# Attention by blocks of 128 queries instead of units of 64, beside the projections on one core

## The chip, the cores and the metric

The kernel runs on one core of one Trainium2 chip. The metric is the device time of one execution in microseconds; the median of 3 runs before is 797.51 us (797.22 to 797.78). Engines are called as the profile calls them: PE multiplies matrices, DVE, ACT and POOL work on tiles, SP issues most of the DMAs.

## The reference, cut to what matters

One layer of a trunk: attention with a sliding window of 128 keys over 512 positions, 32 query heads of 64 in 4 groups that share keys and values, then a gated output product, then a second gated product with an embedding. All in float32.

```python
def swa_mixer(h, w_in, w_out, sinks, rel_bias):
    q, k, v, gate = jnp.split(h @ w_in, [...], axis=-1)
    ...                                   # 4 blocks of 128 queries, each sees 256 keys
    scores = einsum(q, kb) * HEAD_DIM ** -0.5 + bias
    scores = where(mask, scores, min)     # a query sees itself and the 127 keys before it
    m = maximum(scores.max(-1), sink)
    e = exp(scores - m)
    probs = e / (e.sum(-1) + exp(sink - m))
    out = einsum(probs, vb)
    return (out * silu(gate)) @ w_out

def reference(x, p, ...):
    x = x + swa_mixer(rmsnorm(x, norm_g), ...)
    emb = p @ ple_proj
    x = x + emb * sigmoid(rmsnorm(x, ple_norm) @ ple_gate)
    return rmsnorm(x, final_g)
```

## The kernel before, in words

Each float32 operand of a large product is split in a high and a low part (a cast on ACT, a subtraction on DVE), and each product is three matmuls of 128x128 weights with 512 columns (`mm3`, lines 126 to 128). The work has four stages: a first pass over the input that makes keys, values and the first two query projections (to 71 us), then 30 projections with attention beside them (to about 455 us), then the output product, then the second gated product.

A projection is 16 steps of three matmuls (`projections`, a generator: `next(proj)` issues one step). A tile of split weights serves 8 steps. `Weights.get` asks for the split two tiles ahead; `W.todo` holds the splits that were asked for and not issued yet (`_make`: the cast at line 109, the subtraction at line 110). There are three buffers of each. When a projection ends, its result has to leave its bank: three chores go to the list `chores`, for a query projection a scaling on DVE (L312), two casts on ACT (L321) and two subtractions on DVE (L319), for a gate a product on DVE (L600), a tanh on ACT (L601) and a product on DVE (L594). `idle` holds work without haste.

The list `kinds` sets the order of the 14 query and 16 gate projections; `q_at` gives the places of the query projections. Two of them make the queries `Q[d]` of four heads, and there are 8 such `d`.

Attention goes by units of 64 queries and four heads, 64 units in all. A unit passes three generators:

- `scores`: two score products on PE into a bank each (L462), the sink into the tile `t` on POOL (L474); then the bias added, both parts summed, the folded keys merged and the maximum taken on DVE (L487 to L491); then two exponentials on ACT (L495); then the reciprocal of the sums on DVE (L497); then two scalings on ACT that write the tile `pr` (L506).
- `turn`: two transposes of `pr` on PE (L515), a cast on ACT (L520) and a subtraction on DVE (L521) that split the result into `r`; then, but for the first units of a `d`, a masked copy `own` on POOL (L531) and a copy between its halves on ACT (L541).
- `weigh`: two or three value products on PE (L557, L559); after each second unit, two copies on ACT (L568) and two additions on DVE (L570) empty the bank `o` into `U`.

In this stage every engine's order is the order of the program text (`manual_schedule` for PE, SP, DVE, ACT and POOL), so each engine takes its instructions as the loop issues them. In iteration `i` of the loop (from L828) stand, in this order: transposes of unit i-2, value products of unit i-3, score products of unit i, the reciprocal and scalings of unit i-1, the sums of unit i. Then come about 7 projection steps, between which chores, exponentials and copies are issued. `sum_weights` issues the DMAs that add weight tiles for later stages, on SP and POOL.

The tiles `r`, `own` have two buffers, `t` and `pr` three. Of the eight banks, two each belong to projections (tag p), transposes (t), outputs (o) and scores.

Of the kernel before, what the change touches and what calls it, by code (L numbers as in the profile page):

```python
# [11 lines left out]
F32 = mybir.dt.float32  # L12
F32R = mybir.dt.float32r
AF = mybir.ActivationFunctionType
ALU = mybir.AluOpType
# [15 lines left out]
UNITS = S // HB  # L31
# [9 lines left out]
WARM = 24  # L41
XW = S + 1 + 768
# [13 lines left out]
def trunk_kernel(ctx: ExitStack, tc: tile.TileContext, a: dict):  # L56
# [11 lines left out]
    others = {"s": banks_s.enter_context(tc.tile_pool(name="psum_s", bufs=2, space=PSUM))}  # L68
# [112 lines left out]
    q_at = {int(0.5 + 3.516 * (c // 2)) - 3 + c % 2: c for c in range(2, PAIRS)}  # L181
# [214 lines left out]
    spsum = mid.enter_context(tc.tile_pool(name="psum_w", bufs=1, space=PSUM))  # L396
# [7 lines left out]
    U, T, PT, O, gates, biases = {}, {}, {}, {}, {}, {}  # L404
# [41 lines left out]
    def scores(i):  # L446

        d, g = divmod(i, UNITS)
        if g == 4 and d + 1 < TWOS:
            load_bias(d + 1)
        key = K[d // 2]

        s_ps = spsum.tile([P, 2, S], F32, tag="w", name=f"s{i}")
        number = [min(2 * g + u + 1, 5) * QB for u in range(2)]
        for u in range(2):
            first, n = max(2 * g + u - 4, 0) * QB, number[u]  # L460
            st = Q[d][:, 2 * g + u].rearrange("p h q -> p (h q)")
            nc.tensor.matmul(s_ps[:, u, : 2 * n], st, key[:, :, first : first + n], start=True, stop=True)  # L462
        W = KEYS + 2
        t = apool.tile([P, 2, W], F32, tag="t", name=f"t{i}", bufs=3)
        at = t[:, 0, 0:1]

        def two(of, stride, n):
            return bass.AP(tensor=at.tensor, offset=at.offset + of, ap=[at.ap[0], [stride, 2], [1, n]])

        late = QB if g >= 2 else 0  # L470
        seen = [t[:, 0, 0 : P + 1], t[:, 1, 1 + late : P + 2 + late] if late else t[:, 1, 0 : P + 1]]
        both = two(0, W + 1 + late if late else W, P + 1)
        pr = [t[:, u, 1 + late * u : 1 + late * u + P] for u in range(2)]
        nc.gpsimd.tensor_copy(two(0, W + W - 1 if late else W, 1), sinkb[:, d : d + 1].unsqueeze(1).to_broadcast([P, 2, 1]))  # L474
        for u, n in enumerate(number):
            if n < P:
                nc.gpsimd.memset(t[:, u, 1 + n : 1 + P], MASKED)
        yield
        bias = biases[d][:, ::-1]
        if g < 2:  # L480
            for u, n in enumerate(number):
                nc.vector.tensor_add(t[:, u, 1 : 1 + n], s_ps[:, u, :n], bias[:, KEYS - n :])
            for u, n in enumerate(number):
                nc.vector.tensor_add(t[:, u, 1 : 1 + n], s_ps[:, u, n : 2 * n], t[:, u, 1 : 1 + n])
        else:
            x = t[:, :, 1 : 1 + KEYS]
            nc.vector.tensor_add(x, s_ps[:, :, :KEYS], bias.unsqueeze(1).to_broadcast([P, 2, KEYS]))  # L487
            nc.vector.tensor_add(x, s_ps[:, :, KEYS : 2 * KEYS], x)
            nc.vector.tensor_max(two(1, W + P, QB), t[:, :, 1 : 1 + QB], t[:, :, 1 + P : 1 + KEYS])
        sm = apool.tile([P, 24], F32, tag="sm", name=f"sm{i}", bufs=4)  # L490
        nc.vector.tensor_reduce(sm[:, 0:2], both, axis=AX.X, op=ALU.max, negate=True)  # L491
        yield
        for u in range(2):
            su = seen[u]
            nc.scalar.activation(su, su, AF.Exp, bias=sm[:, u : u + 1], accum_out=sm[:, 2 + u : 3 + u])  # L495
        yield
        nc.vector.reciprocal(sm[:, 4:6], sm[:, 2:4])  # L497
        yield

        T[i] = apool.tile([P, 2, P], F32, tag="pr", name=f"pr{i}", bufs=3)  # L500
        for u in range(2):
            out, src = T[i][:, u], pr[u]
            if late and (g + u) % 2:
                out = out.rearrange("p (h k) -> p h k", h=2)[:, ::-1]
                src = src.rearrange("p (h k) -> p h k", h=2)
            nc.scalar.mul(out, src, sm[:, 4 + u : 5 + u])  # L506

    def turn(i):


        d, g = divmod(i, UNITS)
        pr = T.pop(i)
        pt = bank(f"pt{i}", "t")[:, :256]
        for u in range(2):
            nc.tensor.transpose(pt[:, u * P : (u + 1) * P], pr[:, u, :], ident)  # L515

        r = apool.tile([P, 2, 256], F32R, tag="r", name=f"r{i}", bufs=2)
        rh, rl = (r[:, l].rearrange("p (h u q) -> p u h q", h=4, u=2) for l in range(2))
        src = pt.rearrange("p (u h q) -> p u h q", u=2, h=4)
        nc.scalar.copy(rh, src)  # L520
        nc.vector.tensor_sub(rl, src, rh.bitcast(F32))  # L521
        yield
        own = None
        if g >= 2:
            own = apool.tile([P, 2, 256], F32R, tag="own", name=f"own{i}", bufs=2)
            rows = slice(0, P) if g % 2 else slice(0, HB)
            flat = lambda v: v[rows].rearrange("p l (u q) -> p (l u) q", q=HB)


            sign = -1 if g % 2 else 1  # L530
            nc.gpsimd.affine_select(  # L531
                out=flat(own), in_=flat(r).bitcast(F32), pattern=[[0, 8], [sign, HB]], compare_op=ALU.is_ge, fill=0.0,
                base=-HB - 1 if g % 2 else 0, channel_multiplier=-sign,
            )
        PT[i] = (r, own)
        yield
        if own is not None:
            here, there = slice(HB, P), slice(0, HB)
            if g % 2 == 0:
                here, there = there, here  # L540
            nc.scalar.copy(own[there, 0], own[here, 1].bitcast(F32))  # L541

    def weigh(i):

        d, g = divmod(i, UNITS)
        n, b = divmod(g, 2)
        kv = d // 2
        r, own = PT.pop(i)
        if g == 0:
# [3 lines left out]
        ops = O[d]  # L553
        out = ops[:, b].rearrange("p u e q -> p (u e q)")
        first = V[0 if n == 0 else n - 1 + b][:, kv]
        for low in range(2):
            nc.tensor.matmul(out, first, r[:, low], start=low == 0, stop=own is None and low == 1)  # L557
        if own is not None:
            nc.tensor.matmul(  # L559
                out, DV[:, n - 1, b, kv * 2 * HD : (kv + 1) * 2 * HD], own[:, 0], start=False, stop=True  # L560
            )
        yield
        if b:
            dst = U[d][:, :, n * P : (n + 1) * P].rearrange("p u (b q) -> p b u q", b=2)
            lower, upper = slice(0, 64), slice(64, 128)
            tmp = [apool.tile([P, 2, 2, HB], F32, tag=f"tmp{e}", name=f"tmp{e}_{i}", bufs=1) for e in range(2)]
            for e, (o, x) in enumerate(((lower, upper), (upper, lower))):
                nc.scalar.copy(tmp[e][o], ops[x, :, :, e, :])  # L568
            for e, o in enumerate((lower, upper)):
                nc.vector.tensor_add(dst[o], ops[o, :, :, e, :], tmp[e][o])  # L570
        if g == UNITS - 1:
# [248 lines left out]
    blocks = TWOS * UNITS  # L820
# [6 lines left out]
    softmax = iter(())  # L827
    for i in range(blocks + 3):  # L828

        before, softmax = softmax, scores(i) if i < blocks else iter(())  # L830
        turned = turn(i - 2) if 2 <= i < blocks + 2 else iter(())
        value = weigh(i - 3) if 3 <= i else iter(())
        next(turned, None)
        next(value, None)
        next(softmax, None)
        next(turned, None)
        next(before, None)
        next(softmax, None)
        first_chores(i, 0)
        if i in (6, 20, 36):  # L840
            idle.extend(make_key(1 + i // 16))
        todo = left // (blocks + 2 - i) if i < blocks + 2 else 0
        left -= todo
        for n in range(max(todo, 6)):
            if n < todo:
                next(proj)
            if n == 0:
                first_chores(i, 1)
                some(W.todo)
                some(chores or idle)  # L850
            elif n == 2:
                next(value, None)
                if len(chores) > 1:
                    some(chores)
            elif n == 3:
                next(turned, None)
                next(softmax, None)
            elif n == 4:
                first_chores(i, 2)
                some(chores or idle)  # L860
            elif n == 5:
                next(softmax, None)
        if i < blocks:
            for n in range(i * SUM_STEPS // blocks, (i + 1) * SUM_STEPS // blocks):
                sum_weights(n)
# [6 lines left out]
    others["s"] = pool("psum_s2", space=PSUM, bufs=2, reuse_waits="tile")  # L872
# [433 lines left out]
```

## Time and profile before

| what | us |
|---|---|
| median of 3 runs | 797.51 |
| the profiled execution's own time | 797.26 |
| its span, first to last instruction | 795.3 |
| PE busy | 785.0 |
| DVE busy | 587.3 |
| ACT busy | 500.6 |
| POOL busy | 116.2 |

The span is the time between the first and the last instruction of the profiled execution; its own time is longer by what lies around them. Busy times are sums over instructions. A row of the groups reads: line, engine, operation, tiles written and read, shapes and count, then busy time and the mean in ns, then idle time before the group and what ended it. A row in order of time reads: start, duration, engine, line, operation, tiles, shape, how many were merged into the row, and in brackets an idle time before it and who ended it. A row of the windows reads: stretch, then busy time and number of instructions of PE, its weight loads, DVE, ACT and POOL, then the granted clock, DMA share and GB/s.

### The profile page before, as it was taken

What the parts mean: (1) busy time and instruction counts of PE and PEld (TensorE: products, weight loads), DVE (VectorE), ACT (ScalarE), POOL (GpSimd) and SP (SyncE); (2) the same over time, 40 slices, a digit from 0 to 9 for tenths busy, and PEclk for the clock granted to TensorE, in tenths of its full rate; (3) what the DMA queues carried; (4) which work ended last, traced back from release to release, by engine and by line L of the source; (5) the groups of instructions that cost most, each with busy time, mean ns of one, the idle gap of its engine ahead of it and who ended that gap; (6) DMA issues with size and microseconds to landing.
All of it is one profiled execution on the core that took longest, in us unless ns stands there. A gap on an engine that the chain in (4) does not pass through costs nothing.

```text
span 795.3 us, 10980 instructions
## 1 busy us (share of the span) xinstructions
PE 785.0 (99%) x3758; PEld 657.6 (83%) x3758; DVE 587.3 (74%) x1026; ACT 500.6 (63%) x1057; POOL 116.2 (15%) x238
## 2 busy tenths in 40 slices
PE   9999999999999999999999999999999999999995
PEld 8888888888888888888888888888888888888885
DVE  4547697877878597777768898766646757988896
ACT  6643576666767576666757655555568656656765
POOL 0021213131212213121212100030000020200000
PEclk9999999999999999999999999999999999999998
DMA  9983489697869968787875479997603996787633
GB/s 348 271 218 110 117 259 242 172 254 183 226 168 255 206 198 230 192 238 158 247 170 146 119 264 328 352 261 239 205 30 132 373 211 194 159 227 218 180 106 106
DMA packets 42919, 165.28 MB, mean 208 GB/s; under 512 B 6048, under 2 KB 7072, under 8 KB 39024
## 3 DMA queue, kind: packets, MB, share of 16 engines
q1 hardware_dynamic: 35456, 129.67, 48.5%
q0 software_dynamic: 7408, 34.93, 23.9%
q8 instruction: 29, 0.48, 0.2%
q14 instruction: 26, 0.21, 0.1%
HBM read 157.70 MB, written 46.19 MB: 256 GB/s over the span
## 4 chain that ended last, share of the span: by engine, by line
PE 98%; DMA 0%; DVE 0%; ACT 0%; issue 0%; ACTq 0%; DVEq 0%
PE gps L126 7%; PE gps L128 7%; PE gps L127 7%; PE qps L126 7%; PE qps L128 7%; PE qps L127 7%; PE o L126 6%; PE o L128 6%; PE o L127 6%; PE g L126 5%; PE g L127 5%; PE g L128 5%; PE s L462 2%; PE o L557 2%; PE vps L279 2%; PE pt L515 2%
## 5 line engine op out<-in xcount | busy, mean ns | idle before, releaser
L680 DVE TENSOR_TENSOR blo<-braw,bhi 128x1024 fp32r<-128x1024 f32 x80 | 97.8, 1222 | 39.7 <-ACT bhi L679 39.5
L679 ACT CAST bhi<-braw 128x1024 fp32r<-128x1024 f32 x80 | 84.2, 1052 | 65.6 <-PE o L128 19.8
L126 PE MATMUL gps<-xh,whi 128*128 128x512 f32 x256 | 99.9, 390 | 0.1
L128 PE MATMUL gps<-xh,wlo 128*128 128x512 f32 x256 | 99.9, 390 | 0.0
L127 PE MATMUL gps<-xl,whi 128*128 128x512 f32 x256 | 99.8, 390 | 0.0
L126 PE MATMUL o<-bhi,fho 128*128 128x512 f32 x224 | 87.7, 392 | 0.0
L126 PE MATMUL qps<-xh,whi 128*128 128x512 f32 x224 | 87.7, 391 | 0.0
L128 PE MATMUL qps<-xh,wlo 128*128 128x512 f32 x224 | 87.4, 390 | 0.0
L127 PE MATMUL qps<-xl,whi 128*128 128x512 f32 x224 | 87.3, 390 | 0.0
L128 PE MATMUL o<-bhi,flo 128*128 128x512 f32 x224 | 87.2, 389 | 0.0
L127 PE MATMUL o<-blo,fho 128*128 128x512 f32 x224 | 87.2, 389 | 0.0
L110 DVE TENSOR_TENSOR wlo<-wraw,whi 128x1024 fp32r<-128x1024 f32 x60 | 73.8, 1231 | 2.7 <-ACT whi L109 2.4
L126 PE MATMUL g<-bhi,fhg 128*128 128x512 f32 x192 | 75.1, 391 | 0.0
L128 PE MATMUL g<-bhi,flg 128*128 128x512 f32 x192 | 74.8, 389 | 0.0
L127 PE MATMUL g<-blo,fhg 128*128 128x512 f32 x192 | 74.7, 389 | 0.0
L531 POOL TENSOR_SCALAR_AFFINE_SELECT own<-r 64x512 fp32r<-64x512 f32 (+1 forms) x48 | 32.5, 677 | 255.8 <-DVE r L521 255.8
L520 ACT CAST r<-pt 128x256 fp32r<-128x256 f32 x64 | 23.8, 371 | 71.5 <-PE pt L515 71.1
L521 DVE TENSOR_TENSOR r<-pt,r 128x256 fp32r<-128x256 f32 x64 | 27.1, 424 | 55.5 <-ACT r L520 54.8
L109 ACT CAST whi<-wraw 128x1024 fp32r<-128x1024 f32 x60 | 62.4, 1041 | 5.3 <-issue 3.9
L680 DVE TENSOR_TENSOR blo<-grown,bhi 128x1024 fp32r<-128x1024 f32 x32 | 39.1, 1224 | 23.5 <-ACT bhi L679 23.4
L128 PEld LDWEIGHTS gps<-xh,wlo 128*128 128x128 f32 x256 | 48.0, 188 | 10.1
L126 PEld LDWEIGHTS gps<-xh,whi 128*128 128x128 f32 x256 | 48.1, 188 | 9.4 <-PE vps L279 0.5
(207 smaller groups left out, 1736.5 us busy)
## 6 DMA issues: line engine op xcount, KB each, us to landing
wraw<-in_w_gate_in SPq DMA_DIRECT2D x32, 512.0 KB, 5.7
wraw<-in_w_q SPq DMA_DIRECT2D x28, 512.0 KB, 5.0
w_out<-in_w_out POOLq DMA_DIRECT2D x24, 512.0 KB, 7.1
braw<-in_w_out SPq DMA_DIRECT2D x24, 512.0 KB, 4.0
braw<-in_ple_gate SPq DMA_DIRECT2D x24, 512.0 KB, 4.2
xw<-in_first SPq DMA_DIRECT2D x14, 640.5 KB, 6.5
w_out<-in_w_out SPq DMA_DIRECT2D x16, 512.0 KB, 5.8
ple_gate<-in_ple_gate SPq DMA_DIRECT2D x16, 512.0 KB, 6.6
```

The costliest lines, as they stand in the source:

```text
L109: nc.scalar.copy(hi, raw)
L110: nc.vector.tensor_sub(lo, raw, hi.bitcast(F32))
L126: nc.tensor.matmul(ps, sh, mh, start=first, stop=False, skip_group_check=more)
L127: nc.tensor.matmul(ps, sh, ml, start=False, stop=False, skip_group_check=more)
L128: nc.tensor.matmul(ps, sl, mh, start=False, stop=last, skip_group_check=more)
L279: nc.tensor.matmul(v_ps[t], h[:, c], both[:, :, 256:512], start=f, stop=e, skip_group_check=True)
L462: nc.tensor.matmul(s_ps[:, u, : 2 * n], st, key[:, :, first : first + n], start=True, stop=True)
L520: nc.scalar.copy(rh, src)
L521: nc.vector.tensor_sub(rl, src, rh.bitcast(F32))
L531: nc.gpsimd.affine_select(out=flat(own), in_=flat(r).bitcast(F32), pattern=[[0, 8], [sign, HB]], compare_op=ALU.is_ge, fill=0.0, base=-HB ...
L679: nc.scalar.copy(hi, raw)
L680: nc.vector.tensor_sub(lo, raw, hi.bitcast(F32))
```

## The change

Attention goes by blocks of 128 queries: 32 blocks instead of 64 units, each with four score products, four transposes and four to six value products. Block j's iteration starts with the transposes of block j-1, the value products of block j-2 and the score products of block j, one behind the other, then come ACT's cast, DVE's subtraction and POOL's `own` of block j-1 and the sums of block j, and then 13 or 14 projection steps. Behind step 3 stand the exponentials, behind step 4 the copies of `own`, behind step 5 the reciprocal and the emptying of the output bank, behind step 6 the scalings. Splits of weights are taken from `W.todo` at steps 0 and 5; the one of step 5 stands ahead of the reciprocal and the scalings. Chores go out at steps 0, 2, 4, 7, 9 and 11. Scores take four banks, transposes and outputs one each; `r`, `own` and `pr` have one buffer and `t` two. DVE's and the casts' tiles of attention are twice as wide; exponentials, scalings and copies are as many and as wide as before. The places of query projections follow 3.41 instead of 3.516.

The diff, cut (the sums of the first block of a `d`, which go key range by key range as before, the masks, and names only):

```diff
+HALF = 7
...
-    others = {"s": banks_s.enter_context(tc.tile_pool(name="psum_s", bufs=2, space=PSUM))}
+    others = dict.fromkeys("sto", banks_s.enter_context(tc.tile_pool(name="psum_s", bufs=2, space=PSUM)))
...
-    q_at = {int(0.5 + 3.516 * (c // 2)) - 3 + c % 2: c for c in range(2, PAIRS)}
+    q_at = {int(0.5 + 3.41 * (c // 2)) - 3 + c % 2: c for c in range(2, PAIRS)}
...
-    spsum = mid.enter_context(tc.tile_pool(name="psum_w", bufs=1, space=PSUM))
+    spsum = mid.enter_context(tc.tile_pool(name="psum_w", bufs=1, space=PSUM, reuse_waits="tile"))
+    others.update(dict.fromkeys("to", spsum))
...
     def scores(i):
-        d, g = divmod(i, UNITS)
+        d, n = divmod(i, NB)
...
-        s_ps = spsum.tile([P, 2, S], F32, tag="w", name=f"s{i}")
+        s_ps = spsum.tile([P, 4, S], F32, tag="w", name=f"s{i}")
...
-        t = apool.tile([P, 2, W], F32, tag="t", name=f"t{i}", bufs=3)
+        t = apool.tile([P, 4, W], F32, tag="t", name=f"t{i}", bufs=2)
...
-            nc.vector.tensor_add(x, s_ps[:, :, :KEYS], bias.unsqueeze(1).to_broadcast([P, 2, KEYS]))
+            nc.vector.tensor_add(x, s_ps[:, :, :KEYS], bias.unsqueeze(1).to_broadcast([P, 4, KEYS]))
             nc.vector.tensor_add(x, s_ps[:, :, KEYS : 2 * KEYS], x)
...
         yield
-        for u in range(2):
-            su = seen[u]
-            nc.scalar.activation(su, su, AF.Exp, bias=sm[:, u : u + 1], accum_out=sm[:, 2 + u : 3 + u])
+        for v, sv in enumerate(seen):
+            nc.scalar.activation(sv, sv, AF.Exp, bias=sm[:, v : v + 1], accum_out=sm[:, 4 + v : 5 + v])
         yield
-        nc.vector.reciprocal(sm[:, 4:6], sm[:, 2:4])
+        nc.vector.reciprocal(sm[:, 8:12], sm[:, 4:8])
         yield
-        T[i] = apool.tile([P, 2, P], F32, tag="pr", name=f"pr{i}", bufs=3)
-        for u in range(2):
+        T[i] = apool.tile([P, 4, P], F32, tag="pr", name=f"pr{i}", bufs=1)
+        for v in range(4):
...
     def turn(i):
-        pt = bank(f"pt{i}", "t")[:, :256]
-        for u in range(2):
-            nc.tensor.transpose(pt[:, u * P : (u + 1) * P], pr[:, u, :], ident)
-        r = apool.tile([P, 2, 256], F32R, tag="r", name=f"r{i}", bufs=2)
+        pt = bank(f"pt{i}", "t")
+        for v in range(4):
+            c = 2 * (v % 2) + v // 2
+            nc.tensor.transpose(pt[:, c * P : (c + 1) * P], pr[:, v, :], ident)
+        yield
+        r = apool.tile([P, 2, 512], F32R, tag="r", name=f"r{i}", bufs=1)
...
     def weigh(i):
-        if b == 0:
-            O[d] = bank(f"o{i}", "o").rearrange("p (b u e q) -> p b u e q", b=2, u=2, e=2)
+        ops = bank(f"o{i}", "o").rearrange("p (b u e q) -> p b u e q", b=2, u=2, e=2)
+        for b in range(2):
...
-    softmax = iter(())
-    for i in range(blocks + 3):
-        before, softmax = softmax, scores(i) if i < blocks else iter(())
-        turned = turn(i - 2) if 2 <= i < blocks + 2 else iter(())
-        value = weigh(i - 3) if 3 <= i else iter(())
...
+    for j in range(blocks + 2):
+        softmax = scores(j) if j < blocks else iter(())
+        turned = turn(j - 1) if 1 <= j <= blocks else iter(())
+        value = weigh(j - 2) if 2 <= j else iter(())
+        for part in (turned, value, softmax, turned, turned, softmax):
+            next(part, None)
+        todo = left // (blocks + 2 - j)
         left -= todo
-        for n in range(max(todo, 6)):
+        for n in range(max(todo, 2 * HALF)):
+            h, at = divmod(n, HALF)
+            i = 2 * j + h
             if n < todo:
                 next(proj)
-            if n == 0:
+            if n in (0, 5):
+                some(W.todo)
+            if at == 0 and h < 2:
+                if i in (6, 20, 36):
+                    idle.extend(make_key(1 + i // 16))
+                first_chores(i, 0)
                 first_chores(i, 1)
-                some(W.todo)
                 some(chores or idle)
-            elif n == 2:
...
+            elif at == 2 and len(chores) > 1:
+                some(chores)
+            elif at == 4:
                 first_chores(i, 2)
                 some(chores or idle)
-            elif n == 5:
-                next(softmax, None)
...
+            for part in {3: (softmax,), 4: (turned,), 5: (softmax, value), 6: (softmax,)}.get(n, ()):
+                next(part, None)
+            if at == 4 and h < 2 and j < blocks:
+                sums(i)
...
-    others["s"] = pool("psum_s2", space=PSUM, bufs=2, reuse_waits="tile")
+    others.update(dict.fromkeys("sto", pool("psum_s2", space=PSUM, bufs=2, reuse_waits="tile")))
```

More of the change, by code (lines that the diff above doesn't have):

```diff
@@ L463, in scores @@
+        number = [min(4 * n + v + 1, 5) * QB for v in range(4)]
+        for v in range(4):
+            first, c = max(4 * n + v - 4, 0) * QB, number[v]
+            st = Q[d][:, 4 * n + v].rearrange("p h q -> p (h q)")
+            nc.tensor.matmul(s_ps[:, v, : 2 * c], st, key[:, :, first : first + c], start=True, stop=True)
         W = KEYS + 2
[L464 removed]
+        t = apool.tile([P, 4, W], F32, tag="t", name=f"t{i}", bufs=2)
         at = t[:, 0, 0:1]
[L467 to L468 removed]
@@ L470, in scores, with four @@
[L470 to L477, printed above, removed]
+        def four(of, stride, c):
+            return bass.AP(tensor=at.tensor, offset=at.offset + of, ap=[at.ap[0], [2 * W, 2], [stride, 2], [1, c]])
@@ new lines, in scores @@
+        late = QB if n else 0
+        seen = [t[:, v, 1 + late : P + 2 + late] if late and v % 2 else t[:, v, 0 : P + 1] for v in range(4)]
+        pr = [t[:, v, 1 + late * (v % 2) : 1 + late * (v % 2) + P] for v in range(4)]
+        nc.gpsimd.tensor_copy(
+            four(0, W + W - 1 if late else W, 1),
+            sinkb[:, d : d + 1].unsqueeze(1).unsqueeze(1).to_broadcast([P, 2, 2, 1]),
+        )
+        for v, c in enumerate(number):
+            if c < P:
+                nc.gpsimd.memset(t[:, v, 1 + c : 1 + P], MASKED)
@@ L536, in turn @@
         yield
-        if own is not None:
+        for b in range(2 if n else 0):
             here, there = slice(HB, P), slice(0, HB)
-            if g % 2 == 0:
+            if b == 0:
                 here, there = there, here
-            nc.scalar.copy(own[there, 0], own[here, 1].bitcast(F32))
+            nc.scalar.copy(own[b][there, 0], own[b][here, 1].bitcast(F32))
     def weigh(i):
-        d, g = divmod(i, UNITS)
-        n, b = divmod(g, 2)
+        d, n = divmod(i, NB)
         kv = d // 2
@@ L548, in weigh @@
         r, own = PT.pop(i)
-        if g == 0:
+        if n == 0:
             U[d] = apool.tile([P, 2, S], F32, tag="u", name=f"u{d}", bufs=3)
-        if b == 0:
-            O[d] = bank(f"o{i}", "o").rearrange("p (b u e q) -> p b u e q", b=2, u=2, e=2)
[L553 to L561, printed above, removed]
-        yield
[L563 to L570, printed above, removed]
@@ L571, in weigh @@
-        if g == UNITS - 1:
+        ops = bank(f"o{i}", "o").rearrange("p (b u e q) -> p b u e q", b=2, u=2, e=2)
+        for b in range(2):
+            out = ops[:, b].rearrange("p u e q -> p (u e q)")
+            first = V[0 if n == 0 else n - 1 + b][:, kv]
+            for low in range(2):
+                nc.tensor.matmul(
+                    out, first, r[:, low, 256 * b : 256 * b + 256], start=low == 0, stop=not n and low == 1
+                )
+            if n:
+                nc.tensor.matmul(
+                    out, DV[:, n - 1, b, kv * 2 * HD : (kv + 1) * 2 * HD], own[b][:, 0], start=False, stop=True
+                )
@@ L819, in trunk_kernel @@
             W.todo.pop(0)()
-    blocks = TWOS * UNITS
+    blocks = TWOS * NB
     left = KC * (len(kinds) - 1)
@@ L825, in some, with sums @@
             of.pop(0)()
-    softmax = iter(())
-    for i in range(blocks + 3):
-        before, softmax = softmax, scores(i) if i < blocks else iter(())
-        turned = turn(i - 2) if 2 <= i < blocks + 2 else iter(())
-        value = weigh(i - 3) if 3 <= i else iter(())
-        next(turned, None)
-        next(value, None)
-        next(softmax, None)
[L836 to L842, printed above, removed]
+    def sums(i):
+        for n in range(i * SUM_STEPS // (2 * blocks), (i + 1) * SUM_STEPS // (2 * blocks)):
+            sum_weights(n)
```

79 lines of the change are left out of this document (38 added, 41 removed).

## The prediction

> **What bounds the kernel now.** I read the page first (engines, then the chain that ended last), then the windows of 40 us, then the order of time of each engine around one unit of attention. The page:
>
> ```profile
> PE 785.0 (99%) x3758; PEld 657.6 (83%) x3758; DVE 587.3 (74%) x1026; ACT 500.6 (63%) x1057; POOL 116.2 (15%) x238
> ...
> PE 98%; DMA 0%; DVE 0%; ACT 0%; issue 0%; ACTq 0%; DVEq 0%
> ```
>
> A window in the middle of attention:
>
> ```profile
> 240.00:280.00 40.00, 40.00 (x199) 33.69 (x199) 28.94 (x67) 25.83 (x73) 9.54 (x22) 1.00 0.91 226
> ```
>
> PE is busy in 40.00 of 40.00 us at clock 1.00, DVE in 28.94, ACT in 25.83. So attention costs what PE's instructions cost, and nothing else is late. Two questions are left: does PE's own work shrink, and does a new wait reach PE? For the first, one unit's short products (PE in order of time; the last row is PE's weight loads):
>
> ```profile
> 242.78 0.40 PE L128 MATMUL gps<-xh,wlo 128*128 128x512 f32 x1
> 243.01 0.38 PE L515 MATMUL pt<-ident,pr 128*128 128x128 f32 x2
> 243.15 0.48 PE L557 MATMUL o<-r,V 128*128 128x256 f32 x2
> 243.47 0.28 PE L559 MATMUL o<-own,DV 128*128 128x256 f32 x1
> 243.58 0.46 PE L462 MATMUL s<-k,q 128*128 128x320 f32 x2
> 243.88 0.39 PE L126 MATMUL gps<-xh,whi 128*128 128x512 f32 x1
> ...
> 249.54 0.39 PE L126 MATMUL gps<-xh,whi 128*128 128x512 f32 x1
> ```
>
> ```profile
> 242.78 0.37 PEld L515 LDWEIGHTS pt<-ident,pr 128*128 128x128 f32 x2
> ```
>
> From 243.88 to 249.54 a unit takes 5.66: 7 projection steps of 3 matmuls, 21 x 0.227 = 4.77, and 0.89 for two transposes, three value products and two score products. Within the group a value product takes 0.12 (243.47 to 243.58), a score product 0.15, a transpose 0.11 (two end 0.38 after the first began, one lasts 0.27).
>
> **The change, part by part.** *PE's work.* A block of 128 queries issues exactly what two units issued: 4 transposes, 4 to 6 value products, 4 score products of the same columns. Only the number of groups falls, from 67 to 34. What a group costs beyond its products is small: the 0.89 less the products' own 2 x 0.11 + 3 x 0.12 + 2 x 0.15 = 0.88, 0.01 to 0.02. At 0.02, 33 groups save 0.7 us. A block with 14 steps then lasts 2 x 5.66 - 0.02 = 11.30, one with 13 steps 10.62; the quota `left // (blocks + 2 - j)` gives 13 to blocks 0 to 11 and 14 to the rest. A block whose value products belong to the first 128 queries of a `d` lacks two of them: 0.24 less.
>
> *The lag.* Before, a unit's scaled weights were made at the head of the next unit and transposed one unit later still, 5.66 us on, so no lateness on ACT or DVE reached PE. Now block j's transposes take what ACT scaled at step 6 of block j-1: a closed loop, transposes, ACT cast, DVE subtraction, score sums, exponentials, reciprocal, scalings, transposes. With `r` down to one buffer the cast also waits until the last value product that reads the old `r`. If the loop is longer than the block, PE stands still. Its terms (ACT by form, 120 to 440 us; then DVE in order of time):
>
> ```profile
> L109 ACT CAST whi<-wraw 128x1024 fp32r<-128x1024 f32 x50 | 52.0, 1039 | 0.0
> ...
> L506 ACT ACTIVATE pr<-t,sm 128x128 f32<-128x128 f32 x114 | 39.7, 397 | 4.3 <-DVE sm L497 4.1
> L520 ACT CAST r<-pt 128x256 fp32r<-128x256 f32 x58 | 21.5, 371 | 65.0 <-PE pt L515 64.7
> ...
> L541 ACT CAST own<-own 64x256 fp32r<-64x256 f32 x43 | 17.3, 403 | 2.3 <-POOL own L531 1.8
> L321 ACT CAST q<-qps 64x512 fp32r<-64x512 f32 x24 | 13.9, 581 | 13.0 <-DVE qps L312 12.9
> L601 ACT ACTIVATE gps<-gate 128x512 f32<-128x512 f32 x13 | 7.8, 600 | 14.9 <-DVE gate L600 14.9
> ```
>
> ```profile
> 227.11 0.42 DVE L521 TENSOR_TENSOR r<-pt,r 128x256 fp32r<-128x256 f32 x1 [0.49 <-ACT r L520]
> 227.45 0.48 DVE L487 TENSOR_TENSOR t<-s,bias 128x320 f32<-128x320 f32 x1
> 227.97 0.49 DVE L488 TENSOR_TENSOR t<-s,t 128x320 f32<-128x320 f32 x1
> 228.49 0.23 DVE L489 TENSOR_TENSOR t<-t 128x64 f32<-128x64 f32 x1
> 228.75 0.42 DVE L491 TENSOR_REDUCE sm<-t 128x2 f32<-128x258 f32 x1
> 229.09 1.22 DVE L110 TENSOR_TENSOR wlo<-wraw,whi 128x1024 fp32r<-128x1024 f32 x1
> 230.22 0.85 DVE L570 TENSOR_TENSOR u<-o,tmp 64x256 f32<-64x256 f32 x2
> ```
>
> The double widths are not in the trace. They lie on the line through 320 columns (0.48) and 1024 (1.22), 1.05 ns a column (64 columns come out at 0.21, measured 0.23): 640 columns take 0.81, the 516-column reduction 0.69, the 512-column subtraction 0.69; the 512-column cast lies between 0.371 and 1.039, at 0.59. Doubling each instead would add 0.7 to the score sums; the line is the nearer. A start follows its releaser's end by 0.04 (below), and the next of a queue starts up to 0.1 before its predecessor's end (229.09 + 1.22 against 230.22), so scalings follow each other by 0.30, exponentials by 0.40 (225.45 to 225.86, below).
>
> Now a block with own-block products, in us from its first transpose. Fifth value product ends: 4 x 0.11 + 4 x 0.12 + 0.28 = 1.19. Cast 1.23 to 1.82; subtraction from 1.86; sums from 2.47, 0.84 + 0.86 + 0.32 + 0.69, to 5.19. Four exponentials at 0.40, from 5.23 to 6.92; two own copies to 7.45. Then, where a second split of weights is due at step 5, it stands ahead of reciprocal and scalings: ACT's cast to 8.5, DVE's subtraction from 8.55, reciprocal 9.68 to 9.84, four scalings at 0.30 from 9.88 to 11.18, and 0.23 for hand-over and weight load: the last transpose can start at 11.41. PE wants it at 11.30 + 0.32 = 11.62 after 14 steps, at 10.94 after 13. So the second split alone makes a short block 0.47 late and leaves a long one 0.2. Without it the scalings end before 9.5 and nothing is late.
>
> *Where more stands in the loop.* Chores go out at steps 0, 2, 4 in code order, so a DVE chore sits behind the sums and the first split, and an ACT chore that needs it sits in front of the exponentials. Before shows this pattern, DVE then ACT:
>
> ```profile
> 223.10 0.69 DVE L312 SCALAR_TENSOR_TENSOR qps<-qps,rb 128x512 f32<-128x512 f32 x1
> ...
> 226.45 0.17 DVE L497 RECIPROCAL sm<-sm 128x2 f32<-128x2 f32 x1
> ```
>
> ```profile
> 223.82 1.17 ACT L321 CAST q<-qps 64x512 fp32r<-64x512 f32 x2 [1.75 <-DVE qps L312]
> 225.02 0.41 ACT L541 CAST own<-own 64x256 fp32r<-64x256 f32 x1
> 225.45 0.41 ACT L495 ACTIVATE t<-t,sm 128x129 f32<-128x129 f32 x1
> ...
> 225.86 0.39 ACT L495 ACTIVATE t<-t,sm 128x129 f32<-128x129 f32 x1
> ```
>
> The casts waited for the scaling of q and the exponentials for the casts, harmless then. Which blocks are hit follows from counting steps: block j begins at step 16 + 13j (from block 12 on 172 + 14(j - 12)); a split is asked for at each multiple of 8 and served at steps 0 and 5 of a block, a projection ends ahead of each multiple of 16. 22 of the 32 blocks get a second split. Lateness:
> - 18 and 26: q's scaling served at step 0, its casts at step 2. Scaling 6.12 to 6.82 (behind sums and first split), casts to 8.05, exponentials from 7.96 instead of 5.23: late by 2.77 each.
> - 11 (13 steps): a gate's product and tanh in the same places, exponentials from 7.47: 2.7.
> - 6 (13 steps): q's casts at step 4, behind the exponentials: 1.85.
> - 19 and 27: tanh at step 4: 0.44 each. 3 and 7: 0.47 each; 4 and 15: 0.15 together.
> - 1: no value products and a block of 9.92, but q's casts at step 4 and a second split: last transpose ready at 11.4, due at 10.22: 1.2. 0: sums to 3.1, first split, q's scaling to 4.85, casts to 6.1, then the table load, exponentials to 9.0, ready at 10.76, due at 9.79: 1.0. The load:
>
> ```profile
> 83.04 1.28 ACT L601 ACT_TABLE_LOAD   x1
> ```
>
> Sum 5.5 + 2.7 + 1.85 + 0.9 + 0.95 + 0.15 + 2.2 = 14.2 us of PE standing still. Everything else stays covered: the split made at step 0 is done at 6.3 and its first use is at step 8, 7.2; the output bank is emptied about 0.9 after the reciprocal, ahead of the next value products; scores need four banks at the start, freed when the last values are read, ahead of their turn. Fewer instructions on DVE (0.6 us a block) are in the sums above. The queries' earlier places shift projections with the blocks and cost nothing.
>
> Total: 797.26 (the profiled execution: span 795.3 and 1.96 around it; the median is 0.25 above) - 0.7 + 14.2 = 810.8, put at 811.
>
> *Bounds.* If `r`'s release doesn't hold the cast, each loop is 0.57 shorter: 4.3 less. If transposes wait for all four scalings rather than for their own: 0.32 more in each of 11 blocks and 0.1 in some nine others, 4.5 more. If the table load goes out early, 1.0 less. An error of 0.2 in the loop is 2 to 3 us.
>
> **The clock.** A standing PE could lose its clock. The tail shows when:
>
> ```profile
> 785.83 0.28 PE L128 MATMUL e<-bhi,pTl 128*128 128x256 f32 x1
> ```
>
> ```profile
> 787.00:788.00 1.00, 0.00 (x0) 0.00 (x0) 0.91 (x4) 0.88 (x2) 0.00 (x0) 1.00 0.00 0
> 788.00:789.00 1.00, 0.00 (x0) 0.00 (x0) 0.73 (x4) 0.62 (x3) 0.00 (x0) 0.78 0.00 0
> ```
>
> PE ended at 786.1; 0.78 from 788 to 789, read as a fall to half speed, puts it at 788.56, 2.45 us later. The Trainium skill (TensorE: Matmul & The Clock Gate, Why this matters for your kernels) asks only for no gap over about 3 us; by it the sum stays as it is, and this row speaks for an earlier fall.
>
> **The rivals.** 1. *The three long waits (2.7 to 2.8) cost the clock too.* No row shows how long half speed would last; taken as long as the fall took, 2.45 us, each loses 1.2: 811 + 3.7 = 814.7. For it: the row above. Against: the windows may lie otherwise, and PE never paused so in attention before.
> 2. *The loop is shorter than I think* (`r` not holding the cast, exponentials and copies overlapping more): only the long waits remain, 806.
> 3. *Not slower: the loop closes in time.* The lag between step 6, at 5.9 us, and the next transposes, 11.3, is 5.4 us, and the rows give 4.0 for scalings behind a second split in a plain block. If ACT and DVE reach the reciprocal by 9.0 in the loaded blocks too, nothing stands still: 797.26 - 0.7 = 796.6. It decides at a loop of 10.6. For it: a plain long block already holds. Against: ACT's order above, casts ahead of exponentials, 2.7 us in blocks 18 and 26.
>
> **How the numbers follow.** Forecast 0.58, rival 1 0.13, rival 2 0.18, rival 3 0.11. A measurement of this kernel tells 0.2%, 1.6 us, from no change. Rival 3 gives 0.06 within it and 0.05 faster; the other three are slower, 0.89. The range runs from below rival 2, 803.5, to 817.5 (the forecast with transposes waiting for all four, or rival 1 with some error); rival 3 lies outside.
>
> **What would show it.** Right: PE's idle time in attention about 14 us, ended by ACT's scalings (`pr`) at the transposes, the longest 2.7 to 2.8 us in blocks 11, 18, 26; chain of waits with ACT and DVE shares; matmul counts as before; ACT waiting for q's scaling in front of exponentials. Wrong: PE at 40.00 of 40.00 in attention's windows (rival 3), a clock under 1.00 there (rival 1), or waits at other instructions, value products or projections.

## The result and the profile after

The changed kernel takes 816.8 us, the median of 5 runs (816.19 to 818.31), against 797.54 before (797.22 to 797.98): ratio 1.0246, 95% interval 1.0231 to 1.0261. The forecast was 811, its range 803.5 to 817.5; the two longest of the five runs, 818.23 and 818.31, lie above it. The profiled execution took 816.8 us, span 815.1.

The page of the changed kernel, the rows that answer to those of before:

```profile
PE 795.7 (98%) x3758; PEld 661.1 (81%) x3758; DVE 566.5 (69%) x858; ACT 497.6 (61%) x1025; POOL 114.9 (14%) x206
...
PE 87%; DVE 6%; ACT 5%; issue 2%; ACTq 0%; DVEq 0%
```

PE has the same 3758 instructions. DVE lost 20.8 us of work and ACT 3.0, and yet both entered the chain that ended last, with 6% and 5%. The waits name the place (engine, line, who was waited for; us in total, times, longest; the two PE rows overlap):

```profile
ACT t L502 <- DVE sm L496: 62.3, 28, 3.3
DVE wlo L111 <- ACT whi L110: 48.5, 25, 3.1
...
PEld pt L525 <- ACT pr L514: 18.5, 44, 2.8
...
PE pt L525 <- ACT pr L514: 9.1, 6, 2.3
```

In attention PE and its weight loads wait for one thing, the scalings, ahead of the transposes. (A group is the short products at the head of an iteration: group j has the transposes of block j-1.) In order of time PE shows it, first the four transposes of block 2 in group 3 (on time), then those of block 18 in group 19:

```profile
114.09 0.60 PE L525 MATMUL pt<-ident,pr 128*128 128x128 f32 x4
```

```profile
295.26 0.39 PE L129 MATMUL gps<-xh,wlo 128*128 128x512 f32 x1
298.00 1.20 PE L525 MATMUL pt<-ident,pr 128*128 128x128 f32 x4 [2.35 <-ACT pr L514]
298.98 0.48 PE L567 MATMUL o<-r,V 128*128 128x256 f32 x2
```

The wait has two parts: an idle time, and four transposes that come 0.3 us apart, as ACT scales, instead of 0.11. The second part counts as busy, because one transpose lasts 0.27 in the records. So the 9.1 us of idle PE are only about half of what is lost. Measured by starts, the last transpose of a group, due 0.56 after the start of the last projection matmul (0.23 and 3 x 0.11), comes late by (us, by the block that is transposed):

| block | 0 | 1 | 3 | 4 and 15 | 6 | 7 | 11 | 18 | 19 | 26 | 27 | 14, 22, 23, 30, 31 | sum |
|---|---|---|---|---|---|---|---|---|---|---|---|---|---|
| forecast | 1.0 | 1.2 | 0.47 | 0.15 together | 1.85 | 0.47 | 2.7 | 2.77 | 0.44 | 2.77 | 0.44 | 0 | 14.2 |
| measured | 0.6 | 1.1 | 0.8 | 0.2 and 1.2 | 1.9 | 0.8 | 3.0 | 3.05 | 0.1 | 3.05 | 0.75 | 0.7 in all | 17.2 |

The windows behind the wait of block 18, granted clock in the column before the DMA share:

```profile
298.00:299.00 1.00, 1.00 (x5) 0.54 (x5) 0.34 (x1) 0.98 (x4) 0.00 (x0) 1.00 0.42 152
299.00:300.00 1.00, 1.00 (x9) 1.00 (x10) 0.00 (x0) 0.99 (x2) 0.00 (x0) 0.96 1.00 233
300.00:301.00 1.00, 1.00 (x5) 1.00 (x4) 0.86 (x2) 0.95 (x3) 0.00 (x0) 0.50 1.72 631
...
303.00:305.00 2.00, 2.00 (x10) 1.59 (x9) 1.93 (x4) 0.02 (x1) 1.77 (x6) 0.92 0.00 0
```

The two windows left out have 0.50 as well. By 0.96 in the second row and 0.92 in the last, the half clock lasted from 299.9 to 303.3; 3.4 us at half clock cost PE another 1.7 us (whether that was a loss in the end is taken up under the clock, below). Attention, from the first score product to the first matmul of the output stage, took 369.9 us before (81.95 to 451.82) and 389.0 after (82.63 to 471.64). The 0.7 left of the span's 19.8 lies ahead of attention; that stretch varied by as much among the runs below (81.93 to 82.82 for that first product).

### The profile page after: what moved, and what is told of

It is laid out like the page before. It is cut to its first block, busy times and chain, and to the rows that moved or that the text cites. A ratio compares the mean times of both kernels' runs of the same rounds, so it can differ in the third digit from the quotient of the medians.

```text
span 815.1 us, 10808 instructions
## 1 busy us (share of the span) xinstructions
PE 795.7 (98%) x3758; PEld 661.1 (81%) x3758; DVE 566.5 (69%) x858; ACT 497.6 (61%) x1025; POOL 114.9 (14%) x206
## 4 chain that ended last, share of the span: by engine, by line
PE 87%; DVE 6%; ACT 5%; issue 2%; ACTq 0%; DVEq 0%
PE qps L127 6%; PE o L127 6%; PE o L128 6%; PE qps L129 6%; PE o L129 6%; PE qps L128 6%; PE g L129 5%; PE g L128 5%; PE g L127 5%; PE gps L127 5%; PE gps L128 5%; PE gps L129 5%; PE pt L525 3%; DVE wlo L111 2%; PE o L567 2%; PE vps L280 2%
## 5 line engine op out<-in xcount | busy, mean ns | idle before, releaser
L502 ACT ACTIVATE t<-t,sm 128x129 f32<-128x129 f32 x128 | 50.0, 393 | 62.4 <-DVE sm L496 62.3
L128 PEld LDWEIGHTS gps<-xl,whi 128*128 128x128 f32 x256 | 48.4, 189 | 9.3
```

The costliest lines, as they stand in the source:

```text
L128: nc.tensor.matmul(ps, sh, ml, start=False, stop=False, skip_group_check=more)
L502: nc.scalar.activation(sv, sv, AF.Exp, bias=sm[:, v : v + 1], accum_out=sm[:, 4 + v : 5 + v])
```

## The experiments

The theory under test: a block's work on ACT and DVE is a closed loop, since it starts from one group's transposes and must end, with the scalings, before the next group's; PE waits where it comes late. The rival: something that lies in the blocks themselves, single buffers, single banks, wider instructions.

**Only the lag undone.** Transposes take block j-2 and values block j-3. Left out of the diff: the two `tmp` copies share one tile here, to make room.

```diff
-    for j in range(blocks + 2):
+    for j in range(blocks + 3):
...
-        turned = turn(j - 1) if 1 <= j <= blocks else iter(())
-        value = weigh(j - 2) if 2 <= j else iter(())
+        turned = turn(j - 2) if 2 <= j < blocks + 2 else iter(())
+        value = weigh(j - 3) if 3 <= j else iter(())
...
-        todo = left // (blocks + 2 - j)
+        todo = left // (blocks + 3 - j)
...
-        T[i] = apool.tile([P, 4, P], F32, tag="pr", name=f"pr{i}", bufs=1)
+        T[i] = apool.tile([P, 4, P], F32, tag="pr", name=f"pr{i}", bufs=2)
```

> Only the lag is undone: block j's iteration transposes block j-2 and takes the values of block j-3, one block later than in the changed kernel, over 35 iterations; pr has two buffers, and the two halves of the copies tmp share one tile to make room. Widths, single banks, single r and own, places of exponentials and splits stay. Theory L: the scalings have a whole block of 10.6 us or more to spare, PE stands still nowhere in attention, and 32 groups fewer than before save 0.3 to 0.7: 796.5 to 798. Rival B (single buffers, single banks, four score banks, wide instructions): still 810 or more.

809.35 (809.23 to 811.64), ratio 1.0151 (1.0136 to 1.0166). This is neither the theory's range nor the rival's: the transposes were never late, but 12 us stayed (809.35 less the 797.3 of the next version), now as waits ahead of the value products, with one stretch of 3.4 us at half clock behind the longest. PE and then DVE in order of time:

```profile
206.93 0.60 PE L525 MATMUL pt<-ident,pr 128*128 128x128 f32 x4
209.75 0.48 PE L567 MATMUL o<-r,V 128*128 128x256 f32 x2 [2.23 <-ACT pr L514]
```

```profile
207.55 1.22 DVE L111 TENSOR_TENSOR wlo<-wraw,whi 128x1024 fp32r<-128x1024 f32 x1 [2.81 <-ACT whi L110]
208.69 0.17 DVE L504 RECIPROCAL sm<-sm 128x4 f32<-128x4 f32 x1
208.78 0.83 DVE L581 TENSOR_TENSOR u<-o,tmp 64x256 f32<-64x256 f32 x2
```

The value products started 0.14 after DVE had emptied the output bank (209.61); the scalings, which the row names, ended only at 210.24 and so did not release them. The bank is emptied behind the reciprocal, behind the second split. So the loop has two exits into PE (places where what it makes is waited for by PE): the scalings, ahead of the transposes, and the emptied output bank, ahead of the value products. With the first opened the second held. My expectation had overlooked it.

**The second exit opened as well.** The output bank is emptied behind step 2.

```diff
-    for part in {3: (softmax,), 4: (turned,), 5: (softmax, value), 6: (softmax,)}.get(n, ()):
+    for part in {2: (value,), 3: (softmax,), 4: (turned,), 5: (softmax,), 6: (softmax,)}.get(n, ()):
```

> The kernel with the lag of two blocks, and in addition the output bank is emptied behind step 2, in front of exponentials and second split, instead of behind the reciprocal. Theory L2 (the loop of a block has two exits into PE, the scalings through the transposes and the emptying of the single output bank through the value products; with the lag of two blocks the second still binds, 2.23 us at 209.75 in that run): with both exits early PE waits nowhere in attention, 796.5 to 798.5. Rival B2 (some other single buffer, r or the transposes' bank, holds PE): stays at 805 to 810.

797.3 (796.55 to 797.89, 11 runs), ratio 0.9993 (0.9984 to 1.0002). A window of it:

```profile
205.00:245.00 40.00, 40.00 (x203) 34.02 (x202) 29.09 (x51) 28.06 (x75) 9.45 (x18) 1.00 0.82 232
```

PE stands still nowhere but for two waits under 0.4 us. Blocks of 128 queries, wide instructions, single banks, one buffer of `r` and `own`, all are still in it: none of these costs time by itself, with this lag. Attention took 369.76 us, 0.11 less than before with those two waits inside, which fits the forecast 0.7 for fewer groups. The time cannot be told from before, so this version does not beat it.

**The second exit alone.** The same edit on the changed kernel, its lag kept.

> One edit on the changed kernel: the output bank is emptied behind step 2 instead of step 5, lag as in the changed kernel. Theory L2: the scalings still come late, behind the second split, so PE waits at the transposes as before; the output copies leave the stretch between second cast and scalings, where ACT waits for the reciprocal anyway: 815 to 818. Rival O2 (the output bank is what binds in the changed kernel too): 805 to 809.

821.08 (820.55 to 822.28), ratio 1.0294 (1.028 to 1.0308): worse than expected. The output copies now stand in front of the exponentials. ACT behind the sums of block 11, 203.98 to 206.70:

```profile
208.47 0.60 ACT L612 ACTIVATE gps<-gate 128x512 f32<-128x512 f32 x1 [4.25 <-DVE gate L611]
209.08 0.75 ACT L579 COPY tmp<-o 64x256 f32<-64x256 f32 x2
209.85 0.41 ACT L502 ACTIVATE t<-t,sm 128x129 f32<-128x129 f32 x1
```

In blocks 11, 18 and 26 ACT is already late there, so the 0.75 goes into the loop: the last transposes of these three came 3.8 late instead of 3.0, and the clock was now lost behind all three. The four kernels form a square: changed 816.8, lag undone alone 809.35, early emptying alone 821.1, both 797.3. Both exits have to be opened.

**The second split behind the scalings.**

```diff
-            if n in (0, 5):
+            if n in (0, 7):
                 some(W.todo)
```

> One edit on the changed kernel: the second split of weights is taken from the list at step 7, behind the scalings, instead of step 5, in front of reciprocal and scalings. Theory L (a closed loop: PE waits at the transposes for scalings that come late round transposes, cast, subtraction, sums, exponentials, second split, reciprocal, scalings): from the end of the own copies to the scalings the changed kernel shows 2.52 us in block 3 (121.95 to 124.47); without the split the output copies (0.76) are left, so each loaded loop is 1.7 us shorter. What stays late: block 0 (0.6, has no second split), 6 (0.3), 11 (1.2), 18 and 26 (1.3 each), 4.7 us in all, no clock loss: 797.5 + 4.7 = 802, 801 to 804. Rival B (PE is held by the single buffers and banks of r, pr, transposes and outputs, whatever stands in the loop): as the changed kernel, 816 to 818.

810.37 (810.19 to 812.89), ratio 1.0165 (1.0148 to 1.0181): 6.4 less than the changed kernel, where I had expected 14.8 (816.8 less 802); the profiled execution kept the clock. Blocks 18 and 26 came nearly as expected (1.2 late, 1.3 expected), but block 3, 0.8 late before, was now 1.6 late, block 22 2.0 instead of 0.2, and the sum of all lateness 13.1 instead of the expected 4.7. DVE in order of time, from the previous block's end:

```profile
114.39 1.23 DVE L111 TENSOR_TENSOR wlo<-wraw,whi 128x1024 fp32r<-128x1024 f32 x1 [1.39 <-ACT whi L110]
115.65 0.69 DVE L611 TENSOR_TENSOR gate<-gps,rb 128x512 f32<-128x512 f32 x1
...
117.01 0.69 DVE L605 SCALAR_TENSOR_TENSOR gate<-gps,gate 128x512 f32<-128x512 f32 x1 [0.34 <-ACT gps L612]
117.62 0.68 DVE L532 TENSOR_TENSOR r<-pt,r 128x512 fp32r<-128x512 f32 x1
```

The subtraction that heads the next block's loop starts 5.0 us behind the group's first transpose (112.60 to 117.62) instead of 1.9 (114.09 to 116.02 in the changed kernel): the split moved ahead of it is still in the loop, one turn further on.

**The loop cleared between sums and scalings.** Splits at steps 2 and 9, chores only at steps 7 to 12, the bank emptied behind step 4.

```diff
-            if n in (0, 5):
+            if n in (2, 9):
                 some(W.todo)
...
-                some(chores or idle)
-            elif at == 2 and len(chores) > 1:
-                some(chores)
...
+            if n in (7, 11):
+                some(chores or idle)
+            elif n in (8, 9, 10, 12):
+                some(chores)
...
+            for part in {3: (softmax,), 4: (turned, value), 5: (softmax,), 6: (softmax,)}.get(n, ()):
```

> On the changed kernel with its lag, nothing stands between sums and scalings but exponentials, own copies, reciprocal and output copies: splits go out at steps 2 and 9, chores only at steps 7 to 12, the output bank is emptied behind step 4. Theory L2: the loop is 1.24 + 0.6 + 3.4 + 1.7 + 0.9 + 0.8 + 1.4 = 10.1 us or less, below 10.6 of a short block, so PE waits only behind block 0 and where q's casts, a split and its subtraction fill the 2.5 us between scalings and next cast: 797 to 801. Rival B2 (single buffers): 805 or more.

854.22 (854.04 to 854.53), ratio 1.0708 (1.0693 to 1.0723): my reading of the stretch behind the scalings as free was wrong by far. ACT and then DVE behind the scalings of block 3, which end at 130.94:

```profile
130.96 1.24 ACT L352 CAST k<-kt 64x512 fp32r<-64x512 f32 x2
132.23 1.05 ACT L110 CAST whi<-wraw 128x1024 fp32r<-128x1024 f32 x1
133.19 0.59 ACT L612 ACTIVATE gps<-gate 128x512 f32<-128x512 f32 x1
133.71 0.58 ACT L531 CAST r<-pt 128x512 fp32r<-128x512 f32 x1
```

```profile
133.31 1.23 DVE L111 TENSOR_TENSOR wlo<-wraw,whi 128x1024 fp32r<-128x1024 f32 x1 [3.03 <-ACT whi L110]
134.46 0.68 DVE L605 SCALAR_TENSOR_TENSOR gate<-gps,gate 128x512 f32<-128x512 f32 x1
135.17 1.39 DVE L350 TENSOR_TENSOR k<-kt,k 64x512 fp32r<-64x512 f32 x2
136.59 0.69 DVE L532 TENSOR_TENSOR r<-pt,r 128x512 fp32r<-128x512 f32 x1
```

5.6 us pass from the scalings to the subtraction, part of it with DVE idle behind ACT and then ACT idle behind DVE. By starts the transposes came 42 us late in all; two projections waited 1.8 us each for the late subtraction of a query's chore, and 24 us of attention ran at half clock. The loop is all that the two engines do in a block, in their written order, with their hand-overs. A piece costs nothing only where its engine waits anyway. In the changed kernel that is so around the first split: it runs on ACT while DVE does the sums, and on DVE while ACT does the exponentials.

**Exponentials ahead of the chore of step 2.**

```diff
-            elif at == 2 and len(chores) > 1:
+            elif at == 2 and h and len(chores) > 1:
                 some(chores)
+            elif n == 3:
+                next(softmax, None)
+                if len(chores) > 1:
+                    some(chores)
...
-            for part in {3: (softmax,), 4: (turned,), 5: (softmax, value), 6: (softmax,)}.get(n, ()):
+            for part in {4: (turned,), 5: (softmax, value), 6: (softmax,)}.get(n, ()):
```

> One edit on the changed kernel: in the first half of a block the chore of step 2 goes out at step 3 behind the exponentials instead of in front of them. Theory L2: it shortens the loop only where an ACT chore stood in front of the exponentials, blocks 11, 18 and 26: tanh or q's casts then run behind the exponentials as in block 6, the wait falls from 2.9 to about 1.3 in 11 and from 3.1 to about 1.7 in 18 and 26, and with no wait over 2.5 the clock stays up, 1.7 us: 4.4 + 1.7 less, 809 to 812. Rival (place within the step order does not matter, only the work in the loop): 815 to 818.

812.14 (811.91 to 812.59), ratio 1.0181 (1.0167 to 1.0195), 0.14 above the expected range. The waits behind 11, 18 and 26 fell to 1.3 each and the clock stayed at 1.00. The place of one chore was worth 4.7 us. Block 19 came 1.7 late instead of 0.1 and block 20 0.6 instead of none, for a reason that has to do with the clock (below): less given back than expected.

**Two buffers of `r`.**

```diff
-        t = apool.tile([P, 4, W], F32, tag="t", name=f"t{i}", bufs=2)
+        t = apool.tile([P, 4, W], F32, tag="t", name=f"t{i}", bufs=1)
-        r = apool.tile([P, 2, 512], F32R, tag="r", name=f"r{i}", bufs=1)
+        r = apool.tile([P, 2, 512], F32R, tag="r", name=f"r{i}", bufs=2)
```

> One edit on the changed kernel: r, the split transposed weights, has two buffers instead of one, so that ACT's cast need not wait for the value products that read the old r; to make room the score tile t has one buffer, whose release (the scalings) comes 2.5 us ahead of its next sums. Theory L: cast at 0.65 instead of 1.24 us behind the first transpose, loop 0.5 shorter from block 2 on, except block 15, where the cast waits for q's casts anyway. Of 17.6 us of standing PE 12.3 stay; the clock is lost perhaps once more: 810 to 812. Rival B (the single buffer of r is what costs): 797 to 801.

813.63 (812.87 to 814.35), ratio 1.0198 (1.0183 to 1.0213). The cast started 0.6 us earlier, released by the transposes:

```profile
114.72 0.59 ACT L531 CAST r<-pt 128x512 fp32r<-128x512 f32 x1 [0.60 <-PE pt L525]
```

So the single `r` is a term of the loop, as forecast, and worth 3.2 us here and not the whole. Blocks 11, 18 and 26 gained 0.5 each, block 1 lost 0.3, and block 19 came 1.8 late instead of 0.1; the run before shows nearly the same of block 19 with two buffers of `t`, so it does not need the one buffer of `t` as its cause. The clock was lost twice here, behind 11 and 26, though these waits were shorter than in the changed kernel. Block 11, PE in order of time:

```profile
210.52 0.39 PE L129 MATMUL gps<-xh,wlo 128*128 128x512 f32 x1
212.68 1.21 PE L525 MATMUL pt<-ident,pr 128*128 128x128 f32 x4 [1.77 <-ACT pr L514]
```

**Values first.**

```diff
-        for part in (turned, value, softmax, turned, turned, softmax):
+        for part in (value, turned, softmax, turned, turned, softmax):
```

> One edit on the changed kernel: of the short products the values stand first, then transposes, then scores. Theory L: transposes are due 0.71 us later in the group, but the values now come first and need the output bank, which DVE empties until 0.6 us before the last scaling ends (125.13 against 125.75 behind block 3), and the cast waits for transposes instead of values, 0.2 later. So the wait moves from the scalings to the output bank and its length hardly changes: 815 to 819. Rival O (the order alone decides; a late loop gains the 0.71): 11 late blocks less 0.5 each and no clock loss, 808 to 811.

817.98 (816.19 to 820.14), ratio 1.0245 (1.0224 to 1.0267): no difference from the changed kernel. The wait moved to the output bank, as the theory has it, PE in order of time:

```profile
299.36 0.77 PE L567 MATMUL o<-r,V 128*128 128x256 f32 x2 [2.82 <-DVE u L581]
```

The time alone does not decide between theory and rival: the profiled execution, 820.14, lost the clock behind three waits for 6.8 us each, the changed kernel's behind one for 3.4. Matmuls in those stretches took some 7.5 us longer than at full clock, against 1.6; without these, attention is 385.5 us (393.0 less 7.5) against 387.4. So the waits did become shorter, by some 2 us, and the clock took that back. What the order would be worth at full clock is not shown.

## Why the prediction was right, point by point

- **PE's own work**: same instructions, 0.7 saved. The kernel with both exits open shows it as far as it can be told (369.76 against 369.87 us of attention, two short waits included).
- **The lag closes a loop, and PE stands still at the transposes**: shown. With the lag undone and the bank emptied early the time is that of before; the blocks hit were the ones counted out, but for 15 and 19 (below), with the three long waits behind 11, 18 and 26.
- **The terms.** For a plain block, 3, in us from its first transpose: cast 1.24 (forecast 1.23), subtraction 1.93 (1.86), sums 2.53 to 5.26 (2.47 to 5.19), exponentials from 5.35 (5.23), second split from 7.89 (7.47 or so), reciprocal 10.12 (9.68), scalings from 10.38 (9.88). The line for the wide instructions held, 0.82 and 0.69 us. The term that was too small is the own copies: they start only when the last exponential's sum is read (121.09) and take 0.83 instead of 0.53. The forecast's own rows had it: 0.403 for one copy, and 0.43 from one to the next start (225.02 to 225.45). DVE to ACT behind the reciprocal took 0.09 (124.38 to 124.47) instead of 0.04; the 0.66 of idle ACT is its wait for that reciprocal:

```profile
121.12 0.83 ACT L553 CAST own<-own 64x256 fp32r<-64x256 f32 x2
121.98 1.05 ACT L110 CAST whi<-wraw 128x1024 fp32r<-128x1024 f32 x1
123.06 0.76 ACT L579 COPY tmp<-o 64x256 f32<-64x256 f32 x2
124.47 1.28 ACT L514 ACTIVATE pr<-t,sm 128x128 f32<-128x128 f32 x4 [0.66 <-DVE sm L504]
```

  The hand-over to PE was 0.06, not 0.23, and gave part of it back. That leaves some 0.3 us in each of blocks 3, 7, 11, 18, 26 and 27, 1.8 of the 3.0 between 14.2 and 17.2; block 15 is another 1.1, and what else came later and earlier evens out.
- **Blocks 15 and 19: the step that failed inside a right sum.** The forecast put chores behind the scalings at nothing. Block 15, forecast at 0.15 together with block 4, came 1.2 late: q's casts and subtractions, served at steps 9 and 11 of block 14, held the next block's subtraction until 252.47. In block 19 the casts of a key did the same, ACT and then DVE:

```profile
298.85 1.25 ACT L352 CAST k<-kt 64x512 fp32r<-64x512 f32 x2
300.12 0.59 ACT L531 CAST r<-pt 128x512 fp32r<-128x512 f32 x1
```

```profile
300.12 1.39 DVE L350 TENSOR_TENSOR k<-kt,k 64x512 fp32r<-64x512 f32 x2 [1.78 <-ACT k L352]
```

  The subtraction started at 301.55, 3.55 behind the first transpose instead of 1.93, and the scalings 12.63 behind it. That is the same 12.63 as in the run with the exponentials ahead, where the block came 1.7 late. Here it came only 0.1 late, instead of the forecast 0.44, because PE itself was slow: the half clock lay in this block's turn. The step failed again, largest, in the experiment with the cleared loop.
- **Everything else stays covered**: the output bank's emptying was put ahead of the next value products and was, in this kernel, because the transposes in front of them wait for something later still. It was a cover by 0.6 us that vanishes with the lag, as the first experiment showed.
- **The clock (rival 1)** had a chance of 0.13 and came in part: one long wait of three in the profiled execution, 1.7 us against the 1.2 taken for each. The fall came at 299.9, some 4.3 us after the last matmul ahead of the wait had ended (295.26 and 0.39), and none came behind two waits of the same idle time, 2.25 and 2.34. The Trainium skill (TensorE: Matmul & The Clock Gate, Why this matters for your kernels) asks only for no gap over about 3 us. The starts here stand 2.7 apart where it was lost (295.26 to 298.00), and with two buffers of `r` it was lost at 2.16 and 2.23 and kept at 2.22, so the measurement sets the mark lower, and length alone does not decide. Nor was it a net loss here: where the clock was lost behind 18 (this kernel and early emptying alone), block 19 came 0.1 late; where it was kept (two buffers of `r`, exponentials ahead), 1.8 and 1.7, and in the latter block 20 0.6. Behind 26 it is the same: block 27 came 0.75 late in the two that kept the clock there and on time in the two that lost it. The slow stretch took about what it covered. That the runs spread from 816.2 to 818.3 by one such loss more or less is not shown: the mean clock was 0.992 in the run of 818.31, but 0.994 in that of 818.23 as in the other three.
- **The sum**: 811 against 816.8. Of the 5.8, 3.0 are larger waits, 1.7 the clock, 0.7 the stretch ahead of attention; 0.4 is not assigned. Since the clock's share stands in for lateness of blocks 19 and 20, the forecast had in the main two things too small: the own copies, and the chores behind the scalings. The loop and its three long waits were right; that the total still fell inside the range, 0.7 below its upper end, owes something to that end's being drawn for other errors.

## What to carry to other kernels

Where one engine is full and its order is written by hand, a lag between a result and its use can be worth more than fewer or wider instructions, as it was here: count the whole turn of the loop, hand-overs and chores included, against the period, and look for every exit into the full engine, since opening one shows only the next. Of work between two engines in fixed order, none is free for standing "behind" the urgent step; it is free only where its engine waits anyway.

## What the runs showed of the hardware that I had not expected

An idle time read from a busy share hides half of such a wait: four transposes at 0.3 us apart with records of 0.27 count as busy. The half clock, once lost behind a wait of 2.7 us, stayed for 3.4 us and took 1.7 of PE's time; behind waits 0.8 us longer (3.5 between the starts, in the kernel with early emptying alone) it was lost three times out of three, and with the values first (3.1 to 3.2 between the starts) three times out of three for 6.8 us.

In all ten traces the clock changed only at marks of one grid: from one change to the next the execution of the changed kernel has 293.546, 3.413 and 505.173 us, which are 86, 1 and 148 times 3.413; with two buffers of `r` it is 61, 1, 51, 1 and 121 times. So whether a wait of 2.2 to 2.7 us loses the clock seems to depend on how it lies to these marks; no run moved a wait against them to show it. And time at half clock is not simply added: where the next turn of the loop is late anyway, the slow PE only fills the wait.
